# The end of the first attention's script: memory logits in pairs, values behind the last pair

## The chip, the core and the metric

The kernel runs on one core of one Trainium2 chip. Times are device microseconds (us) of one execution; the median of three runs is given. A core has TensorE (PE, with its weight loads PEld), VectorE (DVE), ScalarE (ACT), GpSimd (POOL) and SyncE (SP), which here issues the transfers. Each engine works through its own list of instructions in order and waits at semaphores for the others.

## The reference

A trunk of two layers over 512 tokens of width 1024. Layer 0 mixes tokens with differential attention (6 heads), layer 1 with gated linear attention. In both, 4 more heads attend to 256 memory tokens; both outputs are concatenated and go through one output projection. A gated MLP follows each layer. What the change touches is in layer 0:

```python
mix = diff_attention(q, k, v, ...)         # softmax(q0 k0) - lam * softmax(q1 k1), times v, per head
cross = memory_cross_attention(mem_q, ...) # below
x = x + jnp.concatenate([mix, cross], axis=-1) @ w_out[i]

def memory_cross_attention(q, mem, ...):   # q, k normalized per head
    logits = jnp.einsum('bqhd,bkhd->bhqk', q, k)
    p = jax.nn.softmax(logits, axis=-1)
    return jnp.einsum('bhqk,bkhd->bqhd', p, v)
```

## The kernel before

Large products are computed as three products of split operands (hi and lo parts, in fp32r), the attentions' small products in fp32. Activations are held transposed, in 128x512 tiles.

The order of PE's instructions is written out by hand; that of the other engines is made by a scheduler from the dependences. For the first attention the hand order is the string `SCRIPT`. `do` goes through its words. A letter with a number calls a step; a bare number lets `Filler` issue that many us of products from a queue: first the last projections (`gemm`, L329 to L331), then the first part of the output projection (`product`, L350 to L352, added to the residual on DVE by L1076). Costs of the filler are given by hand. Every step issues its PE instructions where it stands, so a step moved in the script is moved on PE.

The steps that matter, with the lines of the profile:

- `L`, with a step number 0 to 14: logits of one step of the differential attention (L736). A step holds one or two blocks of 128 queries of a head. DVE adds the bias and takes the maxima (L743), ACT exponentiates (L746), DVE combines the two softmaxes (L751 to L755). Steps 10 to 14 belong to the last pair of heads, 4 and 5.
- `T`: turns (transposes) such a step's weights on PE (L219); ACT copies them out of PSUM (L765). `V`: times the values (L777). When a head's last block is done, ACT squares its output (L788) for the norm.
- `s`, with a head's number: closes that norm and scales the output on DVE (L796). `F`: transposes the head's output (L219) and splits it on ACT (L309) and DVE (L310) into an operand of the output projection.
- `k0`, `k1`: transposes of the memory keys of layer 0 and of layer 1 (L219, copied by ACT, L577). `q1`: transposes of the memory queries (L219, copied by ACT, L599).
- `l`, with a block's number 0 to 3: memory logits of one block of 128 queries (L608), then its softmax: maxima on DVE (L616), four exponentials on ACT (L620), reciprocal and scaling on DVE (L622, L624). Each block gives two tiles of weights.
- `t`, with a tile's number 0 to 7: transposes of one of these tiles (L219), copied by DVE (even numbers) or ACT (odd ones), both L633.
- `v0`, `v1`: memory values for two blocks each (L646), 64 columns of the array at a time, and the split of the result (L309 and L310, tiles mxh and mxl). Each of these two operands of the output projection is whole only after `v1`.
- `O`: gives the filler the second part of the output projection, first those products that do not use head 5, of these first heads 3 and 4 (xsh, xsl) and then the memory heads (mxh, mxl). `!` empties the filler.

PSUM has eight banks, under four tags of two each: `mm` (projections), `lg`, `sm`, `tp` (transposes). A step that takes a bank waits on PE until the bank's former content has been read. Weights come through SP's transfers into raw tiles, are split by ACT (cast, L252) and DVE (L255) and held in six pairs of tiles; a pair is freed when the product that used it last has ended. The last projection before the output projection is that of layer 1's memory keys and values; ACT empties its banks (L568 and L569).

Of the kernel before, what the change touches and what calls it, by code (L numbers as in the profile page):

```python
# [48 lines left out]
    L9 V7 P4 b2 4.45 T8 T9 s2 3.0  # L49
    L10 V8 3.55 X P5 q0  # L50
    L11 b3 V9 T10 4.2
    L12 F2 V10 s3 T11 3.8 q1 k0
    L13 3.15 l0 V11 T12 3.65
    L14 F3 t0 3.3 V12 T13 t1 l1 3.9 T14 l2 t2 2.3 O k1 t3 s4 l3 v0 t4 V13 V14 t6 t5 1.3 t7 F4 v1 s5 F5 6.15 ! 4.55
"""

ORDER = (('v', 0), ('qk', 1), ('kv', 0), ('qk', 2), ('vm', 2), ('kv', 1))
# [28 lines left out]
def _pieces():  # L86

    plan = []

    def piece(key, name, i, ks, *ranges):  # L90
        plan.append((key, name, i, ks, ranges))

    for l in range(2):
        if l == 0:
            w = "w_in_diff"
            piece(("qk", 0), w, 0, K8, (0, 256), (768, 1024))
            for key in ORDER:
                if key[0] == "qk":
                    p = key[1]
                    piece(key, w, 0, K8, (256 * p, 256 * p + 256), (768 + 256 * p, 1024 + 256 * p))  # L100
                elif key[0] == "kv":
                    piece(key, "w_mem_kv", key[1], K8, (0, 512))
                elif key[0] == "vm":
                    p = key[1]
                    piece(key, w, 0, K8, (1536 + 256 * p, 1792 + 256 * p), (2304, 2560))
                else:
                    p = key[1]
                    piece(key, w, 0, K8, (1536 + 256 * p, 2048 + 256 * p))
        else:
            w = "w_in_gla"  # L110
            piece(("gm", 1), w, 0, K8, (2304, 2576))
            for c in range(5):
                piece(("g", c), w, 0, K8, (512 * c, min(512 * c + 512, 2304)))
        for i, part in enumerate(PASS[l]):
            for c, ks in part:
                piece(("o", l, i, c), "w_out", l, ks, (256 * c, 256 * c + 256))
        base = 0
        for nq in HALVES:
            for q in range(base, base + nq):
                piece(("ua", l, q), "w_up", l, K8, (256 * q, 256 * q + 256))  # L120
                piece(("ug", l, q), "w_up", l, K8, (DFF + 256 * q, DFF + 256 * q + 256))
            for c in range(4):
                piece(("dn", l, base, c), "w_down", l, tuple(range(2 * base, 2 * base + 2 * nq)),
                      (256 * c, 256 * c + 256))
            base += nq
    return plan


def _blocks():

    out = []
    for key, name, i, ks, ranges in _pieces():
        w = sum(b - a for a, b in ranges)
        step = WTILE // w
        out.append([(name, i, ks[j:j + step], ranges, w) for j in range(0, len(ks), step)])
    return out
# [42 lines left out]
def trunk(ctx, tc, head_d, x_t, mem_t, wpack, cols_a_d, cols_d, conv_d, gate_d, rel_bias, diff_lambda, consts, onehot, out):  # L179
# [12 lines left out]
    def bank(tag):  # L192
        return ps.tile([128, 512], F32, name=f"ps_{tag}", tag=tag)

    def xtile():
        return xs.tile([128, S], F32, name="xt", tag="xs", bufs=XS)
# [9 lines left out]
    def blk(b, w=128):  # L206
        return slice(w * b, w * b + w)
# [40 lines left out]
    plan, blocks, made = _pieces(), _blocks(), []  # L248
# [336 lines left out]
    class MemAttn:  # L585
# [13 lines left out]
                A.activation(self.qT[hp], p, AF.Copy, scale=c_mq(self.l))  # L599


        def logits(self, *blocks):
            banks = [(bank(tag), bank(tag)) for _, tag in zip(blocks, ("lg", "sm") if self.l else ("lg", "tp"))]
            for b, pl in zip(blocks, banks):
                for hp in range(2):
                    for j in range(2):
                        hh = blk(j, 64)
                        mm(pl[j][:, blk(hp, 256)], self.qT[hp][hh, blk(b)], kmT[self.l][hh, hp], start=True, stop=True)  # L608
            for b, pl in zip(blocks, banks):
                self.softmax(b, pl)  # L610
# [51 lines left out]
    def diff_layer(pool, mix, acc):  # L662
# [45 lines left out]
        def members(t):  # L708
            pr, s = divmod(t, len(TOGETHER))
            out, at = [], 0  # L710
            for j, i in TOGETHER[s]:
                out.append((2 * pr + j, i, 4 * j + i, at))
                at += 128 * (i + 1)
            return pr, out, at

        def bias(h):
            bt = heads[h]["bt"] = pool.tile([128, S], F32, name="bt", bufs=2)
            src = bass.AP(tensor=bias_d.tensor, offset=bias_d[h].offset + 1, ap=[[1, 128], [1, 512]])
            nc.sync.dma_start(bt, src)
            G.memset(bt[0:64, 0:64], -1e30)  # L720

        def logits(t, tag="lg"):
            pr, group, _ = members(t)
            P = pairs[pr]
            s2, nm, rc = P["s2"], P["nm"], P["rc"]
            for h, _, _, _ in group:
                if "bt" not in heads[h]:
                    bias(h)
            pls = bank(tag), bank(tag)
            for h, i, _, at in group:  # L730
                nk = 128 * (i + 1)
                cuts = (0, nk) if i == 0 else (0, nk // 2, nk)
                for k0, k1 in zip(cuts, cuts[1:]):
                    for m in range(2):
                        hh = blk(m, 64)
                        mm(pls[m][:, at + k0:at + k1], heads[h]["q"][hh, blk(i)], heads[h]["k"][hh, k0:k1],  # L736
                           start=True, stop=True)
            e = xtile(), xtile()
            for m in range(2):
                for h, i, g, at in group:  # L740
                    c = slice(at, at + 128 * (i + 1))
                    n1 = nm[:, 8 * m + g:8 * m + g + 1]
                    V.tensor_tensor_reduce(  # L743
                        out=e[m][:, c], in0=pls[m][:, c], in1=heads[h]["bt"][:, 127 + 128 * i::-1], scale=-1.0,
                        scalar=1e38, op0=ALU.add, op1=ALU.min, accum_out=n1)
                    A.activation(e[m][:, c], e[m][:, c], AF.Exp, scale=-1.0, bias=n1,  # L746
                                              accum_out=s2[:, m, g:g + 1])
            ids = sorted(g for _, _, g, _ in group)
            step = max(ids[-1] - ids[0], 1)
            b, lr = slice(ids[0], ids[-1] + 1, step), slice(8 + ids[0], 9 + ids[-1], step)  # L750
            V.reciprocal(rc[:, b], s2[:, 1, b])  # L751
            V.scalar_tensor_tensor(rc[:, lr], rc[:, b], nlam, s2[:, 0, b], op0=ALU.mult, op1=ALU.mult)
            for _, i, g, at in group:
                c = slice(at, at + 128 * (i + 1))
                V.scalar_tensor_tensor(e[1][:, c], e[1][:, c], rc[:, 8 + g:9 + g], e[0][:, c],  # L755
                                                    op0=ALU.mult, op1=ALU.add)
            live[t] = e[1]
# [57 lines left out]
        ma = MemAttn(pool, 0, qm, mix, False)  # L815
        ops, keys = [None] * 2, [None] * 2
        for key in ORDER:
# [16 lines left out]

        doing = {
            "L": logits, "M": lambda i: logits(i, "tp"), "T": turn, "V": values, "P": prepare, "F": finish,
            "N": lambda i: norms(i // 2, i % 2), "a": lambda i: ops[0]((2 * i, 2 * i + 1)),
            "b": lambda i: ops[1]((2 * i, 2 * i + 1)), "k": lambda i: keys[i]("sm"),
            "q": lambda i: ma.queries() if i else (F.need("v2"), ma.norm()),
            "l": lambda i: ma.logits(i), "t": ma.turn, "v": lambda i: ma.values(i, "sm"),  # L840
            "s": lambda i: scales.pop(i)(), "X": lambda i: load_x(x_t),
            "O": lambda i: last.append(out_proj(0, mix, 1, acc, 5)), "!": lambda i: F.flush()}
        do(SCRIPT, doing)
# [226 lines left out]
    def load_x(src):  # L1070
        for k in range(KT):
            xT[k] = xtile()
            nc.sync.dma_start(xT[k], src[k])
# [124 lines left out]
    for l in range(2):  # L1198
        with tc.tile_pool(name=f"at{l}", bufs=2) as pool:
            mix = [None] * 8  # L1200
            sums, acc = acc, [None]
            if l == 0:
                diff_layer(pool, mix, acc)
            else:
                gla_layer(pool, mix, sums)
                out_proj(1, mix, len(PASS[1]) - 1, acc)
                F.flush()
        with tc.tile_pool(name=f"ff{l}", bufs=2) as pool:
            acc = ffn(pool, l, acc)
# [73 lines left out]
```

## Time and profile before

| | |
|---|---|
| median of 3 runs | 1165.53 us (1165.47 to 1165.78) |
| profiled execution | 1165.97 us |
| its span, first to last instruction | 1164.1 us |
| DVE busy | 750.9 us (64%) |
| ACT busy | 545.5 us (47%) |
| stretch of the changed steps | about 172 to 226 us |

A row of a timeline gives the start, how long the instruction or the run of equal instructions took, the engine, the line, the operation, the tile written and those read, the shape, and how many there are; in brackets stands the engine's idle time before it and what ended it. Matmuls overlap with those behind them, so the step from one start to the next is what one costs on PE, and a row's own length is a little more. A matmul of fp32 stands as two records, one of fp32r or a transpose as one.

### The profile page before, as it was taken

The page shows a single profiled execution, that of the slowest core. Times are in us where ns is not written, and L with a number is a line of the kernel's source. Part 1 is how long each engine was busy: PE and PEld are TensorE (multiplying, and loading weights), DVE is VectorE, ACT ScalarE, POOL GpSimd, SP SyncE. Part 2 cuts the span into 40 slices and gives each one's busy share as a digit, 9 for nine tenths or more (in the row PEclk, how much of TensorE's full clock was granted, in tenths as well). Part 3 has the DMA queues.
Part 4 walks back from the last instruction along what each step waited for, and adds up shares of the span by engine and source line. Part 5 has one row for each costly group of instructions (what it writes and reads, how often), then busy time and mean ns, then how long its engine had stood idle before and what let it go on. Part 6 is the DMA issues. An engine that isn't in the chain of part 4 may idle for free.

```text
span 1164.1 us, 14796 instructions
## 1 busy us (share of the span) xinstructions
PE 1159.3 (100%) x5656; PEld 966.6 (83%) x5656; DVE 750.9 (64%) x1259; ACT 545.5 (47%) x951; POOL 6.5 (1%) x30
## 2 busy tenths in 40 slices
PE   9999999999999999999999999999999999999998
PEld 7888887888888888888888888988888888888887
DVE  7576778688677326677457637767976733576741
ACT  7676687555344213444337634436543421344420
POOL 0000000000000000000000000000000000000000
PEclk9999999999999999999999999999999999999999
DMA  8422242223223223222341220333332323231221
GB/s 298 162 81 85 77 140 73 72 102 130 76 91 125 83 84 125 73 95 98 121 145 60 99 100 7 114 118 104 105 112 73 108 92 109 90 110 73 91 100 45
DMA packets 39652, 117.76 MB, mean 101 GB/s; under 512 B 4767, under 2 KB 7256, under 8 KB 39582
## 3 DMA queue, kind: packets, MB, share of 16 engines
q1 hardware_dynamic: 39150, 116.44, 29.0%
q8 instruction: 44, 0.72, 0.2%
q10 hardware_dynamic: 432, 0.39, 0.1%
q14 instruction: 26, 0.21, 0.1%
HBM read 112.60 MB, written 4.21 MB: 100 GB/s over the span
## 4 chain that ended last, share of the span: by engine, by line
PE 99%; DMA 0%; ACT 0%; DVE 0%; DVEq 0%; issue 0%
PE ps_mm L350 9%; PE ps_mm L352 9%; PE ps_mm L351 9%; PE ps_sm L352 8%; PE ps_sm L350 8%; PE ps_sm L351 8%; PE ps_mm L329 6%; PE ps_mm L331 6%; PE ps_mm L330 6%; PE ps_tp L352 3%; PE ps_lg L352 3%; PE ps_lg L351 3%; PE ps_tp L351 3%; PE ps_lg L350 3%; PE ps_tp L350 3%; PE ps_tp L219 3%
## 5 line engine op out<-in xcount | busy, mean ns | idle before, releaser
L252 ACT CAST whi<-raw 128x1024 fp32r<-128x1024 f32 (+4 forms) x212 | 207.6, 986 | 247.1 <-PE ps_tp L351 120.9
L255 DVE TENSOR_TENSOR wlo<-raw,whi 128x1024 fp32r<-128x1024 f32 (+4 forms) x212 | 240.4, 1140 | 121.8 <-ACT whi L252 118.6
L350 PE MATMUL ps_mm<-xsh,whi 128*128 128x512 f32 x438 | 171.6, 392 | 0.0
L351 PE MATMUL ps_mm<-xsl,whi 128*128 128x512 f32 x438 | 170.5, 389 | 0.0
L352 PE MATMUL ps_mm<-xsh,wlo 128*128 128x512 f32 x438 | 170.5, 389 | 0.0
L350 PE MATMUL ps_sm<-xsh,whi 128*128 128x512 f32 x378 | 147.0, 389 | 0.0
L351 PE MATMUL ps_sm<-xsl,whi 128*128 128x512 f32 x378 | 147.0, 389 | 0.0
L352 PE MATMUL ps_sm<-xsh,wlo 128*128 128x512 f32 x378 | 147.0, 389 | 0.0
L329 PE MATMUL ps_mm<-whi,xsh 128*128 128x512 f32 (+2 forms) x328 | 126.5, 386 | 0.0
L1130 ACT ACTIVATE cvo<-u,cv 128x512 f32<-128x512 f32 x88 | 71.4, 815 | 112.1 <-DVE u L1128 112.1
L331 PE MATMUL ps_mm<-whi,xsl 128*128 128x512 f32 (+2 forms) x328 | 123.0, 375 | 0.0
L330 PE MATMUL ps_mm<-wlo,xsh 128*128 128x512 f32 (+2 forms) x328 | 122.8, 374 | 0.0
L351 PEld LDWEIGHTS ps_mm<-xsl,whi 128*128 128x128 f32 x438 | 82.3, 188 | 17.2 <-DVE xsl L310 0.4
L352 PEld LDWEIGHTS ps_mm<-xsh,wlo 128*128 128x128 f32 x438 | 82.2, 188 | 17.1
L350 PEld LDWEIGHTS ps_mm<-xsh,whi 128*128 128x128 f32 x438 | 82.2, 188 | 16.9 <-issue 0.3
L1131 DVE SCALAR_TENSOR_TENSOR cvo<-u,cv,cvo 128x512 f32<-128x512 f32 x88 | 65.7, 749 | 36.2 <-ACT cvo L1130 36.0
L351 PEld LDWEIGHTS ps_sm<-xsl,whi 128*128 128x128 f32 x378 | 70.9, 188 | 14.8
L352 PEld LDWEIGHTS ps_sm<-xsh,wlo 128*128 128x128 f32 x378 | 70.9, 188 | 14.7
L350 PEld LDWEIGHTS ps_sm<-xsh,whi 128*128 128x128 f32 x378 | 71.0, 188 | 14.7
L331 PEld LDWEIGHTS ps_mm<-whi,xsl 128*128 128x128 f32 x328 | 61.7, 188 | 11.4
L329 PEld LDWEIGHTS ps_mm<-whi,xsh 128*128 128x128 f32 x328 | 61.7, 188 | 11.0 <-issue 0.7
L330 PEld LDWEIGHTS ps_mm<-wlo,xsh 128*128 128x128 f32 x328 | 61.8, 188 | 10.0
(312 smaller groups left out, 1778.1 us busy)
## 6 DMA issues: line engine op xcount, KB each, us to landing
raw<-in_wpack_dram SPq DMA_DIRECT2D x178, 512.0 KB, 3.5
xt<-in_x_t_dram SPq DMA_DIRECT2D x15, 256.0 KB, 5.4
raw<-in_wpack_dram SPq DMA_DIRECT2D x15, 256.0 KB, 5.1
raw<-in_wpack_dram SPq DMA_DIRECT2D x8, 384.0 KB, 3.4
xres<-xt SPq DMA_DIRECT2D x8, 256.0 KB, 3.6
xt<-xres SPq DMA_DIRECT2D x8, 256.0 KB, 5.4
out_dram<-xt SPq DMA_DIRECT2D x7, 256.0 KB, 2.0
bt<-bias_d SPq DMA_DIRECT2D x6, 256.0 KB, 4.7
```

The lines of the kernel that those rows point to most:

```text
L219: nc.tensor.transpose(dst, src, ident[:n, :n])
L252: ins = A.copy(hi[:, c], raw[:, c])
L255: V.tensor_sub(lo[:, c], raw[:, c], hi[:, c].bitcast(F32))
L329: mm(p, sh[k][:, blk(b)], hi, start=k == 0, stop=False)
L330: mm(p, sh[k][:, blk(b)], lo, start=False, stop=False)
L331: mm(p, sl[k][:, blk(b)], hi, start=False, stop=k == KT - 1)
L350: mm(p, hi[:, blk(n)], bh, start=i == first, stop=False)
L351: mm(p, hi[:, blk(n)], bl, start=False, stop=False)
L352: mm(p, lo[:, blk(n)], bh, start=False, stop=i == last)
L1130: A.activation(c, u[:, 2:], AF.Identity, scale=cv[l][:, 2, j:j + 1], bias=cv[l][:, 3, j:j + 1])
L1131: V.scalar_tensor_tensor(c, u[:, 1:S + 1], cv[l][:, 1, j:j + 1], c, op0=ALU.mult, op1=ALU.add)
```

## The change

The last three lines of the script are written anew, and memory logits get a second form, `m`. A block takes two banks of one tag: of `lg` in the form `l`, of `tp` in the form `m`.

```diff
     L11 b3 V9 T10 4.2
-    L12 F2 V10 s3 T11 3.8 q1 k0
-    L13 3.15 l0 V11 T12 3.65
-    L14 F3 t0 3.3 V12 T13 t1 l1 3.9 T14 l2 t2 2.3 O k1 t3 s4 l3 v0 t4 V13 V14 t6 t5 1.3 t7 F4 v1 s5 F5 6.15 ! 4.55
+    L12 F2 V10 s3 T11 2.5 k0 q1 1.3
+    L13 m0 3.15 V11 T12 2.6 t0 t1 1.3
+    L14 m1 3.9 V12 F3 T13 1.3 s4 T14 1.3 k1 t2 F4 1.3 t3 0.65
+    l2 m3 O 1.3 v0 V13 V14 1.3 t4 t5 s5 1.95 t6 t7 F5 0.65 v1 ! 4.55
 """
...
-        def logits(self, *blocks):
-            banks = [(bank(tag), bank(tag)) for _, tag in zip(blocks, ("lg", "sm") if self.l else ("lg", "tp"))]
+        def logits(self, *blocks, tags=None):
+            banks = [(bank(tag), bank(tag)) for _, tag in zip(blocks, tags or (("lg", "sm") if self.l else ("lg", "tp")))]
...
-            "l": lambda i: ma.logits(i), "t": ma.turn, "v": lambda i: ma.values(i, "sm"),
+            "l": lambda i: ma.logits(i), "m": lambda i: ma.logits(i, tags=("tp",)),
+            "t": ma.turn, "v": lambda i: ma.values(i, "sm"),
```

So m0 and m1 stand right behind the logits of steps 13 and 14, m3 right behind l2. The transposes k0 and q1 stand ahead of the last six products of their projection, T12 to T14 and the turns t0 to t7 lie between products in another way, t6, t7 and F5 follow one another, and after v1 the emptied filler goes on at once.

## The prediction

> **What bounds the kernel now.** I read the page first, then the waits of TensorE (PE), then the windows around the changed stretch, 172 to 226 us, and last the timeline of each engine there. The page, its busy times and its chain of waits:
>
> ```profile
> span 1164.1 us, 14796 instructions
> PE 1159.3 (100%) x5656; PEld 966.6 (83%) x5656; DVE 750.9 (64%) x1259; ACT 545.5 (47%) x951; POOL 6.5 (1%) x30
> ...
> PE 99%; DMA 0%; ACT 0%; DVE 0%; DVEq 0%; issue 0%
> ```
>
> The waits of PE, whole (us in total, times, longest):
>
> ```profile
> PE ps_tp L456 <- DVE idle L451: 1.1, 1, 1.1
> ```
>
> The windows (length, busy time of PE, PEld, DVE, ACT and POOL, then granted clock, DMA share, GB/s):
>
> ```profile
> 172.00:195.00 23.00, 23.00 (x142) 18.57 (x141) 19.33 (x49) 17.26 (x49) 0.00 (x0) 1.00 0.20 67
> 195.00:226.00 31.00, 31.00 (x218) 25.88 (x217) 20.52 (x45) 15.63 (x51) 0.00 (x0) 1.00 0.13 43
> ```
>
> PE is busy for 1159.3 of 1164.1 us, the chain that ended last is 99% PE, and the only wait that the view of PE's waits shows in the whole run is 1.1 us at the start. In both windows PE is busy all the time at a granted clock of 1.00, while DVE and ACT have gaps. So the stretch costs what PE's instructions cost one after another. The change adds and removes no arithmetic, so it can gain only at the joints between PE instructions; and it loses whatever wait it opens.
>
> **What the reordering saves on PE.** The logits (L736, L608) use 64 rows of the array, two matmuls side by side. Into such a group and out of it PE loses time. Layer 1 has the paired form already, sixteen L608 records in a row:
>
> ```profile
> 185.98 0.39 PE L352 MATMUL ps_mm<-xsh,wlo 128*128 128x512 f32 x1
> 186.30 1.13 PE L736 MATMUL ps_lg<-kT,qT 64*128 64x256 f32 x8
> ...
> 193.59 1.13 PE L608 MATMUL ps_lg<-kmT,xt 64*128 64x256 f32 x8
> ...
> 194.99 0.39 PE L351 MATMUL ps_mm<-xsl,whi 128*128 128x512 f32 x1
> ...
> 636.25 1.13 PE L608 MATMUL ps_lg<-kmT,xt 64*128 64x256 f32 x8
> ...
> 638.52 0.40 PE L330 MATMUL ps_mm<-wlo,xsh 128*128 128x512 f32 x1
> ```
>
> Going in: products are 0.23 us apart, but 185.98 to 186.30 is 0.32, so 0.09. A lone group of eight records: 193.59 to the second product at 194.99 is 1.40, less that product's own 0.23, is 1.17. Sixteen: 638.52 - 636.25 - 0.23 = 2.04, so the second eight cost 0.87. Pairing saves 1.17 + 0.09 - 0.87 = 0.39 each. The change makes three pairs (m0 behind the L736 of step 13, m1 behind that of step 14, l2 with m3): 1.2. It gives back one joint, since the last logits stood directly ahead of v0 (L646) and no longer do: some 0.2 to 0.25, and up to 0.15 where a lone group stood between transposes, whose way out is cheaper than into products. I take 0.85, bounds 0.5 and 1.2.
>
> The Trainium skill (TensorEngine Tiling (Array Packing), Key Properties) says that a change of tiling mode drains the array while another tile in the same mode does not. The pair at 636.25, with other operands but the same 64 rows, bears it out; if every new operand drained as well, the sum below would be 0.85 us higher.
>
> **What it may uncover.** ACT and DVE run in order, and the changed program's order on them differs: each pair sends its exponentials (L620) down ACT together with those of the differential step. I follow each chain that ends in a PE instruction, with the durations of these rows.
>
> Wait 1, the second bank of the output projection (182.71 before). It takes the bank that the last memory-value product leaves, emptied on ACT by L568 and L569.
>
> ```profile
> 173.98 0.40 PE L331 MATMUL ps_mm<-whi,xsl 128*128 128x512 f32 x1
> ...
> 174.21 1.04 PE L219 MATMUL ps_tp<-C,qm 128*128 128x128 f32 x8
> ...
> 174.41 1.05 ACT L252 CAST whi<-raw 128x1024 fp32r<-128x1024 f32 x1 [0.53 <-PE ps_mm L331]
> ...
> 175.49 1.23 DVE L255 TENSOR_TENSOR wlo<-raw,whi 128x1024 fp32r<-128x1024 f32 x1 [0.61 <-ACT whi L252]
> ...
> 175.62 1.14 PE L736 MATMUL ps_lg<-kT,qT 64*128 64x192 f32 x12
> ...
> 177.39 0.62 ACT L746 ACTIVATE xt<-xt,nmd 128x384 f32<-128x384 f32 x1 [0.19 <-DVE nmd L743]
> ...
> 179.38 0.39 ACT L252 CAST whi<-raw 128x256 fp32r<-128x256 f32 x1
> ...
> 180.04 0.46 ACT L569 ACTIVATE vm<-ps_mm,r_mem 128x256 f32<-128x256 f32 x1
> ...
> 182.71 0.48 PE L350 MATMUL ps_mm<-xsh,whi 128*128 128x512 f32 x1
> ...
> 182.88 0.47 ACT L620 ACTIVATE xt<-ps_lg,nmm 128x256 f32<-128x256 f32 x1
> ...
> 184.69 0.60 ACT L765 COPY xt<-ps_tp 128x512 f32<-128x512 f32 x1
> ```
>
> Before, the cast L252 starts at 174.41, when the product at 173.98 has ended. The change puts the twelve transposes (0.11 each, 174.21 to 175.62 less the 0.09 of going in) ahead of the last six products: that product ends 1.32 later, the cast starts at 175.73, DVE's L255 behind it 1.08 later (as 174.41 to 175.49), at 176.81. The softmax of step 13 on DVE (L743) stands behind L255, 1.23 long; before, the first L746 on ACT came 0.67 after L255's end, so now at 178.71. From there to the 256-wide cast takes 1.99 as before (177.39 to 179.38): 180.70. But now four L620 stand ahead of that cast, 1.81 (182.88 to 184.69): 182.51. Cast, L568 and L569 take 1.12 (179.38 to 180.50): 183.63. PE itself arrives at 182.71 less 0.39 for one pairing, 182.32. That is a wait of 1.3, and a tenth less for each place where an instruction starts before its forerunner's end (rows overlap by nearly 0.1), so 1.1 to 1.4. I take 1.25. Before, the bank was empty at 180.50, 2.2 us early.
>
> A wait also has to be left. Here PE waited for DVE's xsl:
>
> ```profile
> 752.61 0.75 DVE L310 SCALAR_TENSOR_TENSOR xsl<-ps_tp,cols,xsh 128x512 fp32r<-128x512 f32 x1
> ...
> 753.42 0.50 PE L351 MATMUL ps_mm<-xsl,whi 128*128 128x512 f32 x1
> 753.75 0.40 PE L352 MATMUL ps_mm<-xsh,wlo 128*128 128x512 f32 x1
> ```
>
> DVE ends at 753.36, PE starts at 753.42, and the next product follows 0.33 later instead of 0.23: 0.06 + 0.10 = 0.16.
>
> Wait 2, the transposes of step 14 (T14). In the changed program their first one waits for ACT's copy (L765) of T13's, whose bank they take. T13 stands right behind V12 and F3, where ACT still has the four squares L788 of V12.
>
> ```profile
> 189.89 0.67 ACT L309 ACTIVATE xsh<-ps_tp,cols 128x512 fp32r<-128x512 f32 x1
> ...
> 191.73 1.05 PE L777 MATMUL ps_sm<-v,xt 128*128 128x128 f32 x8
> ...
> 192.37 0.37 ACT L788 ACTIVATE xt<-ps_sm,rs 128x128 f32<-128x128 f32 x1 [0.94 <-PE ps_sm L777]
> ...
> 193.76 0.60 ACT L765 COPY xt<-ps_tp 128x512 f32<-128x512 f32 x1
> ...
> 194.23 0.33 ACT L240 ACTIVATE rs_y<-ss,eps 128x4 f32<-128x4 f32 x1
> 194.43 0.60 ACT L633 COPY xt<-ps_tp 128x512 f32<-128x512 f32 x1
> ```
>
> From the start of V12's L777: ACT starts the squares 0.64 later, is through them at 2.03 (193.76), then xsh (L309, 0.67, of which 0.58 count because of the overlap), L240 (0.20 to the next start) and the copy, 0.60: 3.41, with the way out 3.57. PE: 0.89 for L777, 0.80 for eight transposes, 1.45 for six products: 3.14. Wait 0.43; I take 0.45, bounds 0.3 and 0.55.
>
> Wait 3, the transposes of F5. Now t6, t7 and F5 stand in a row, three banks' worth on two `tp` banks, so F5 waits for DVE's copy of t6.
>
> ```profile
> 198.88 0.60 PE L219 MATMUL ps_tp<-C,xt 128*128 128x128 f32 x4
> 199.51 0.59 ACT L765 COPY xt<-ps_tp 128x512 f32<-128x512 f32 x1 [0.29 <-PE ps_tp L219]
> ...
> 202.13 0.68 DVE L633 COPY xt<-ps_tp 128x512 f32<-128x512 f32 x1
> ```
>
> A copy starts 0.63 after the transposes' start (198.88 to 199.51) and takes 0.68 on DVE: 1.31, and 1.47 with the way out. PE comes after eight transposes, 0.87. Wait 0.6, bounds 0.5 and 0.7. Before, products stood between these transposes.
>
> Wait 4, the products of the memory heads' output (mxh, mxl), which now follow v1 directly; before, F5 and fifteen products (3.4 us) stood between.
>
> ```profile
> 209.82 0.38 ACT L309 ACTIVATE mxh<-ps_sm 128x256 fp32r<-128x256 f32 x1 [1.02 <-DVE mxl L310]
> ...
> 213.29 1.97 PE L646 MATMUL ps_sm<-xt,vm 128*64 128x128 f32 x32
> ...
> 215.19 0.66 PE L219 MATMUL ps_tp<-C,o 128*128 128x128 f32 x4
> ...
> 215.31 0.38 ACT L309 ACTIVATE mxh<-ps_sm 128x256 fp32r<-128x256 f32 x1 [1.17 <-PE ps_sm L646]
> ...
> 215.72 0.42 DVE L310 SCALAR_TENSOR_TENSOR mxl<-ps_sm,mxh 128x256 fp32r<-128x256 f32 x1 [0.59 <-ACT mxh L309]
> ```
>
> ACT starts mxh 0.12 after PE could go on (215.19); it ends at 215.69. PE starts at 215.75 and needs mxl, which ends at 216.14, so at 216.20, with 0.10 on the next. The second mxh waits for the first mxl (the releaser at 209.82): ACT 216.17 to 216.55, DVE 216.58 to 217.00, PE 217.06. Unhindered, that product (the fifth) would stand at 215.20 + 0.33 + 3 x 0.23 = 216.22; with the tenth for leaving it is 0.95 late. Bounds 0.8 and 1.1.
>
> The rest costs nothing: SP's list of transfers is the same row for row, casts that are up to 2 us later feed products more than 10 us on, and the earlier k0, F4 and s4 are single instructions in ACT's and DVE's gaps. PE's later arrivals do not shorten waits 2 to 4, since each of their chains starts at PE itself.
>
> **Sum.** 1.25 + 0.45 + 0.6 + 0.95 = 3.25, less 0.85: 2.4 us more. The profiled execution took 1165.97 (span 1164.1, 1.87 around it), 0.44 above the median of the runs; 1165.97 + 2.4 - 0.44 = 1167.9. With all bounds to one side 1.5 and 3.25, so about 1167.0 to 1168.8 for this case.
>
> **Rivals.**
> - A fifth wait. F5 needs head 5's `o`, which waits for V14's squares on ACT behind the mxh of v0, L240, L241 and a chain of small DVE steps. By my rows it is ready some 0.4 us before F5 would start, and behind wait 3; but 0.4 us over a dozen steps on two engines is thin. If these queues slip, as each hop of 0.03 to 0.06 allows, another 0.5 to 1.5 comes: 1168.4 to 1169.4.
> - Not slower: ACT is done in time at wait 1. What decides is whether L569 ends before PE arrives, 1.25 us earlier than I have it. Then 2.0 - 0.85 = 1.15 is left, 1166.7, within 0.2%. Against it: the four L620 stand ahead of the evacuation in ACT's order, and 1.81 us of work cannot vanish.
> - Nothing waits, so only the joints count: 1165.53 - 0.85 = 1164.7. It needs all four chains to be over a third shorter than their rows.
> - The clock falls after the waits. Both windows show 1.00. If it halved for the fifteen products behind one wait, 15 x 0.23 = 3.4 more: 1171.3. The Trainium skill (TensorE: Matmul & The Clock Gate, A second HAM failure mode: psum-queue depth-cycling) tells of a kernel whose short idle times between groups made the gate swing. No run here shows that yet, and four waits in 40 us are few.
>
> **How the numbers follow.** A measurement of this kernel can tell about 0.2%, 2.33 us, from no change, and the forecast lies right there. Forecast 0.60, of which 0.36 above 2.33 and 0.24 below; fifth wait 0.28; ACT in time 0.07; nothing waits 0.01; clock 0.03; and 0.01 for a gain past the bound, for which no row speaks. Slower 0.36 + 0.28 + 0.03 = 0.67, same 0.24 + 0.07 + 0.01 = 0.32, faster 0.01. The range leaves out the clock and the ends of the others: 1166.7 to 1169.4.
>
> **What would show it.** PE's waits should list four new ones: L350 for ACT (L569) near 182 us, over 1 us; L219 for ACT's L765 near 197; L219 for DVE's L633 near 216; L350 and L351 for mxh and mxl behind v1. The pairs L736 with L608 should show 0.87 for the second eight. It is wrong if PE shows no wait at L350, if F5 waits for `o`, or if products behind a wait lie more than 0.23 us apart.

## The result and the profile after

The changed kernel takes 1167.99 us (median of 11 runs, 1167.45 to 1170.54), beside 1165.78 for the kernel before in the 11 runs that go with them (1165.21 to 1167.43). The ratio is 1.002, with a 95% interval of 1.0012 to 1.0028: slower by 0.2%, or 2.2 us by the medians. Forecast were 1167.9 us and 2.4 us of loss. The profiled execution took 1167.99 too.

The page of the changed kernel (span, busy times, chain of waits) and, below it, the waits of PE, whole:

```profile
span 1166.2 us, 14789 instructions
PE 1159.4 (99%) x5656; PEld 965.9 (83%) x5656; DVE 751.3 (64%) x1259; ACT 546.7 (47%) x951; POOL 6.5 (1%) x30
...
PE 98%; ACT 1%; DVE 0%; DMA 0%; issue 0%; DVEq 0%
```

```profile
PE ps_tp L457 <- DVE idle L452: 1.1, 1, 1.1
PE ps_mm L351 <- ACT vm L570: 0.9, 1, 0.9
PE ps_mm L351 <- ACT mxh L310: 0.5, 1, 0.5
PE ps_tp L220 <- DVE xt L634: 0.3, 1, 0.3
PE ps_mm L532 <- ACT xsh L310: 0.2, 1, 0.2
```

PE is as busy as before (1159.4 beside 1159.3 us) in a span that is 2.1 us longer. Line numbers have moved by one: L351 was L350, L220 was L219. Of the new waits three stand in this view, the second one not; it shows on PE's weight load, below. The last row belongs to the first 5 us of the run.

**How large is the loss in one profile?** The time up to 153 us differs between executions, so spans are poor for tenths of a us. Two rows of PE, one ahead of the stretch and one behind it, are better: the first logits near 153 us, and the same product of the output projection near 233 us. Timelines of PE, before and after:

```profile
153.33 1.14 PE L736 MATMUL ps_lg<-kT,qT 64*128 64x192 f32 x12
...
232.70 0.39 PE L350 MATMUL ps_mm<-xsh,whi 128*128 128x512 f32 x1
```

```profile
153.03 1.14 PE L737 MATMUL ps_lg<-kT,qT 64*128 64x192 f32 x12
...
234.77 0.39 PE L351 MATMUL ps_mm<-xsh,whi 128*128 128x512 f32 x1
```

Before, 79.37 us lie between them, after 81.74: the stretch costs 2.37 more. Behind it the distance stays as it is to the end, so all of the loss is there. Every experiment below is measured so, most of them in a single run, and not all on one chip. That the measure can be trusted over runs and chips shows where no edit changes the amount of work: from the first row to the logits of step 13 all thirteen profiles take 22.29 or 22.30 us.

**The four waits.** Timeline of the changed kernel at wait 1 (start, duration, engine):

```profile
175.44 1.05 ACT L253 CAST whi<-raw 128x1024 fp32r<-128x1024 f32 x1
...
176.52 1.23 DVE L256 TENSOR_TENSOR wlo<-raw,whi 128x1024 fp32r<-128x1024 f32 x1 [1.93 <-ACT whi L253]
...
178.25 0.62 ACT L747 ACTIVATE xt<-xt,nmd 128x384 f32<-128x384 f32 x1 [1.77 <-DVE nmd L744]
...
180.25 0.46 ACT L621 ACTIVATE xt<-ps_tp,nmm 128x256 f32<-128x256 f32 x1
...
181.69 0.60 PE L220 MATMUL ps_tp<-C,xt 128*128 128x128 f32 x4
...
182.05 0.41 ACT L253 CAST whi<-raw 128x256 fp32r<-128x256 f32 x1
...
182.71 0.48 ACT L570 ACTIVATE vm<-ps_mm,r_mem 128x256 f32<-128x256 f32 x1
...
183.24 0.50 PE L351 MATMUL ps_mm<-xsh,whi 128*128 128x512 f32 x1 [0.95 <-ACT vm L570]
```

It is the chain of the forecast, link by link, each within 0.2 us of its forecast when counted from the row near 153: late product, late cast, DVE's L256, first exponential of step 13, four L621 of m0 ahead of the 256-wide cast, then the evacuation, which ends at 183.19. PE starts 0.05 behind it. Its transposes at 181.69 were through at 182.05 (four take 0.36 up to a product elsewhere), so the wait is 1.19.

Waits 2 and 3, in the same timeline:

```profile
197.39 0.60 ACT L766 COPY xt<-ps_tp 128x512 f32<-128x512 f32 x1
197.51 0.39 PE L353 MATMUL ps_mm<-xsh,wlo 128*128 128x512 f32 x1
...
198.04 0.42 PEld L220 LDWEIGHTS ps_tp<-C,xt 128*128 128x128 f32 x4 [0.56 <-ACT xt L766]
...
198.45 0.48 PE L351 MATMUL ps_mm<-xsh,whi 128*128 128x512 f32 x1
...
215.24 0.69 DVE L797 TENSOR_TENSOR o<-ps_sm,rs 128x512 f32<-128x512 f32 x1
...
215.48 1.03 PE L220 MATMUL ps_tp<-C,xt 128*128 128x128 f32 x8
216.12 0.69 DVE L634 COPY xt<-ps_tp 128x512 f32<-128x512 f32 x1 [0.18 <-PE ps_tp L220]
...
216.86 0.66 PE L220 MATMUL ps_tp<-C,o 128*128 128x128 f32 x4 [0.35 <-DVE xt L634]
...
217.27 0.48 PE L351 MATMUL ps_sm<-xsh,whi 128*128 128x512 f32 x1
```

T14 starts 0.53 after the product at 197.51 instead of 0.23, when ACT's copy (197.99) is done: 0.30, and its four transposes take 0.41 to the next product instead of 0.36: 0.35 in all. F5 starts at 216.86, when DVE's copy of t6 (216.81) is done; eight transposes from 215.48 take 0.87, so PE could have been there at 216.35: 0.51, and again 0.05 for leaving. Head 5's `o` (L797) was ready at 215.93, so the fifth wait did not come.

Wait 4:

```profile
218.15 1.97 PE L647 MATMUL ps_sm<-xt,vm 128*64 128x128 f32 x32
220.16 0.38 ACT L310 ACTIVATE mxh<-ps_sm 128x256 fp32r<-128x256 f32 x1 [1.92 <-PE ps_sm L647]
220.58 0.42 DVE L311 SCALAR_TENSOR_TENSOR mxl<-ps_sm,mxh 128x256 fp32r<-128x256 f32 x1 [1.55 <-ACT mxh L310]
220.60 0.49 PE L351 MATMUL ps_mm<-mxh,whi 128*128 128x512 f32 x1 [0.48 <-ACT mxh L310]
...
221.06 0.50 PE L352 MATMUL ps_mm<-mxl,whi 128*128 128x512 f32 x1
...
221.46 0.42 DVE L311 SCALAR_TENSOR_TENSOR mxl<-ps_sm,mxh 128x256 fp32r<-128x256 f32 x1 [0.45 <-ACT mxh L310]
...
221.94 0.50 PE L352 MATMUL ps_mm<-mxl,whi 128*128 128x512 f32 x1
...
222.28 0.39 PE L353 MATMUL ps_mm<-mxh,wlo 128*128 128x512 f32 x1
```

The first product waits for mxh (220.54), the second for mxl (221.00), the fifth, at 221.94, for the second mxl (221.88). A block of values takes 1.90 to its successor (213.29 to 215.19 in the kernel before), so PE could have gone on at 220.05, and the fifth product would have stood at 220.05 + 0.33 + 3 x 0.23 = 221.07. It was 0.87 late, and the product behind it follows 0.34 later instead of 0.23: 0.98.

The sum of the waits is 1.19 + 0.35 + 0.56 + 0.98 = 3.08. The stretch lost 2.37, so the joints saved 0.71.

### The profile page after: what moved, and what is told of

Same layout as the page of the kernel before. It is cut to its first block, busy times and chain, and to the rows that moved or that the text cites. A ratio compares the mean times of both kernels' runs of the same rounds, so it can differ in the third digit from the quotient of the medians.

```text
span 1166.2 us, 14789 instructions
## 1 busy us (share of the span) xinstructions
PE 1159.4 (99%) x5656; PEld 965.9 (83%) x5656; DVE 751.3 (64%) x1259; ACT 546.7 (47%) x951; POOL 6.5 (1%) x30
## 4 chain that ended last, share of the span: by engine, by line
PE 98%; ACT 1%; DVE 0%; DMA 0%; issue 0%; DVEq 0%
PE ps_mm L351 9%; PE ps_mm L352 9%; PE ps_mm L353 9%; PE ps_sm L352 8%; PE ps_sm L353 8%; PE ps_sm L351 7%; PE ps_mm L330 6%; PE ps_mm L332 6%; PE ps_mm L331 6%; PE ps_lg L352 3%; PE ps_tp L352 3%; PE ps_tp L353 3%; PE ps_tp L351 3%; PE ps_lg L353 3%; PE ps_lg L351 3%; PE ps_tp L220 3%
## 5 line engine op out<-in xcount | busy, mean ns | idle before, releaser
L256 DVE TENSOR_TENSOR wlo<-raw,whi 128x1024 fp32r<-128x1024 f32 (+4 forms) x212 | 240.4, 1140 | 121.1 <-ACT whi L253 120.3
L351 PE MATMUL ps_mm<-xsh,whi 128*128 128x512 f32 x438 | 172.0, 393 | 0.9 <-ACT vm L570 0.9
L351 PE MATMUL ps_sm<-xsh,whi 128*128 128x512 f32 x378 | 147.1, 389 | 0.0
L330 PE MATMUL ps_mm<-whi,xsh 128*128 128x512 f32 (+2 forms) x328 | 126.6, 386 | 0.0
L351 PEld LDWEIGHTS ps_mm<-xsh,whi 128*128 128x128 f32 x438 | 82.2, 188 | 18.5 <-ACT vm L570 1.2
L351 PEld LDWEIGHTS ps_sm<-xsh,whi 128*128 128x128 f32 x378 | 71.0, 188 | 14.8
L330 PEld LDWEIGHTS ps_mm<-whi,xsh 128*128 128x128 f32 x328 | 61.7, 188 | 11.2 <-issue 1.0
```

Of the source, the lines that this page charges most:

```text
L256: V.tensor_sub(lo[:, c], raw[:, c], hi[:, c].bitcast(F32))
L330: mm(p, sh[k][:, blk(b)], hi, start=k == 0, stop=False)
L351: mm(p, hi[:, blk(n)], bh, start=i == first, stop=False)
```

## The experiments

Three other theories stood beside the forecast's (four waits, each with its own chain, less what the joints save). A: there is one lateness of ACT and DVE, which begins at wait 1 and comes out again wherever PE next needs one of them. B and C: wait 1 is made by the pair alone, or by the late product alone. D: the pairs save less than their rows said. What was measured, with the starts of the two rows of PE:

| run | row near 153 | row near 233 | stretch against before |
|---|---|---|---|
| before | 153.33 | 232.70 | |
| changed | 153.03 | 234.77 | +2.37 |
| F5 behind three products | 152.83 | 233.98 | +1.78 |
| v1 earlier | 152.79 | 232.98 | +0.82 |
| products ahead of T14 | 152.85 | 234.19 | +1.97 |
| k0, q1 back, m0 single | 153.44 | 234.59 | +1.78 |
| k0, q1 back | 153.57 | 234.90 | +1.96 |
| m0 single | 153.05 | 234.30 | +1.88 |
| first two lines alone | 153.41 | 233.64 | +0.86 |
| all waits covered | 152.48 | 231.55 | -0.30 |
| the same without pairs | 152.61 | 232.45 | +0.47 |
| the same, t0 and t1 late | 152.81 | 231.90 | -0.28 |
| v0 behind the pair | 153.44 | 232.33 | -0.48 |

The edits are in the script; where nothing else is said, they are made to the changed kernel.

**Wait 3 alone.**

```diff
-    l2 m3 O 1.3 v0 V13 V14 1.3 t4 t5 s5 1.95 t6 t7 F5 0.65 v1 ! 4.55
+    l2 m3 O 1.3 v0 V13 V14 1.3 t4 t5 s5 1.95 t6 t7 0.65 F5 v1 ! 4.55
```

> Measure: what the stretch costs on PE against before (+2.36 us in the changed kernel: a PE row near 153 us and one near 233 us, difference of the two). Here the three products that stood between F5 and v1 stand ahead of F5. Theory (four waits of separate chains, less the saved joints): wait 3 (F5 for DVE's copy of t6) goes, the three products that cost 0.69 anyway now cover it, the others stay: +1.85 (2.36 less 0.51). Rival A (one late chain upstream that comes out wherever PE first needs it): F5 or v1 waits in its place, +2.3 to +2.4.

PE's waits in this run, whole:

```profile
PE ps_tp L457 <- DVE idle L452: 1.1, 1, 1.1
PE ps_mm L351 <- ACT vm L570: 0.9, 1, 0.9
PE ps_mm L351 <- ACT mxh L310: 0.5, 1, 0.5
```

The wait for DVE's copy is gone and nothing took its place; the others stand as they were. 0.59 came back, the wait with its slow leaving (0.56). Rival A falls here.

**Waits 3 and 4.**

```diff
-    l2 m3 O 1.3 v0 V13 V14 1.3 t4 t5 s5 1.95 t6 t7 F5 0.65 v1 ! 4.55
+    l2 m3 O 1.3 v0 V13 V14 1.3 t4 t5 s5 1.3 t6 t7 0.65 v1 0.65 F5 0.65 ! 4.55
```

> v1 stands three products behind t7, then three products, F5, three products, and only then the products of mxh and mxl. Theory: waits 3 and 4 both go, 2.36 - 0.51 - 0.97 = +0.9, up to 0.1 more where t4's successors now meet a bank too early. Rival A (the lateness of ACT and DVE comes from waits 1 and 2 and moves on): v1 waits for the copies of t6 and t7 instead, +1.5 or more.

1.55 came back (2.37 - 0.82); the two waits as read from the rows are 1.54.

**Wait 2.**

```diff
-    L14 m1 3.9 V12 F3 T13 1.3 s4 T14 1.3 k1 t2 F4 1.3 t3 0.65
+    L14 m1 3.9 V12 F3 T13 1.95 s4 T14 1.3 t2 F4 1.3 k1 t3
```

> Three products move from behind T14 to between T13 and s4, and k1 moves behind F4, so that T14 comes 0.69 later. Theory: wait 2 (T14 for ACT's copy of T13) goes, measured at 0.30 in the changed kernel; with k1's joint unchanged +2.05 (between 1.8 and 2.1). Rival A: +2.36, a wait of the same size at the next transposes.

0.40 came back, beside 0.35 from the rows. Waits 1, 3 and 4 stayed.

**Wait 1, both of its parts taken back.**

```diff
-    L12 F2 V10 s3 T11 2.5 k0 q1 1.3
-    L13 m0 3.15 V11 T12 2.6 t0 t1 1.3
+    L12 F2 V10 s3 T11 3.8 q1 k0
+    L13 0.65 m0 2.5 V11 T12 2.6 t0 t1 1.3
```

> k0 and q1 go back behind all six products of their projection, and m0 stands one group of three products behind the logits of step 13, no pair. Theory: the product whose evacuation PE waited for is early again and the four exponentials of m0 reach ACT later, so wait 1 (1.19) goes; the pair's joint is paid again (0.2 to 0.39). +1.35 to +1.6; waits 2, 3 and 4 stay as they are, within 0.05. Rival A (waits 2 to 4 are the lateness of wait 1 carried on): they shrink with it, +0.3 or less.

Only 0.59 came back, less than I had expected, though wait 1 is gone and waits 2 to 4 have their size. 1.19 less the pair's 0.39 should be 0.80. The missing 0.2 is a new wait that the view of waits doesn't list. Timelines of PE and DVE of this run, at step 14's pair:

```profile
188.07 1.13 PE L737 MATMUL ps_lg<-kT,qT 64*128 64x256 f32 x8
188.38 0.68 DVE L634 COPY xt<-ps_tp 128x512 f32<-128x512 f32 x1
...
189.03 1.22 PE L609 MATMUL ps_tp<-kmT,xt 64*128 64x256 f32 x8
...
190.18 0.50 PE L351 MATMUL ps_mm<-xsh,whi 128*128 128x512 f32 x1
```

In the changed kernel the same pair takes 1.93 (188.47 to 190.40), here 2.11. m1 takes two `tp` banks; the one of t0 is free only when DVE's copy (L634) ends at 189.06, 0.03 after the group has started on the other bank. In the single records of the trace the first two matmuls, which run side by side, start at 189.03 and 189.12, where in the changed kernel they start 0.01 apart; the later ones stay 0.02 apart. That is 0.18.

**One of the two parts back at a time.**

```diff
-    L12 F2 V10 s3 T11 2.5 k0 q1 1.3
+    L12 F2 V10 s3 T11 3.8 k0 q1
```

> Only k0 and q1 go back behind the six products; the pair of step 13 and m0 stays. Theory: wait 1 (1.19 at L351 for ACT's L570) goes, because the product and with it cast, L256 and the maxima of step 13 are 1.3 early again; but m0 now stands too close behind k0 and q1 and waits for ACT's copies of them, some 0.5 to 0.6 (one copy of 0.59 not covered). +1.6 to +1.8 in the stretch. Rival B (the pair itself causes wait 1, its four exponentials ahead of the evacuation, wherever k0 and q1 stand): L351 still waits 0.8 or more, +2.3 to +2.9.

```diff
-    L13 m0 3.15 V11 T12 2.6 t0 t1 1.3
+    L13 0.65 m0 2.5 V11 T12 2.6 t0 t1 1.3
```

> Only m0 moves, three products behind the logits of step 13; k0 and q1 stay early. Theory: both parts make wait 1, so taking the pair away leaves the late product: the exponentials of m0 come behind the 256-wide cast and the evacuation, the wait falls by 0.8 to 0.9 to some 0.35 and the pair's 0.39 is paid again: +1.8 to +1.95. Rival B (pair alone): the wait goes whole, 2.36 - 1.19 + 0.39 = +1.55. Rival C (the late product alone): the wait stays, +2.7.

Timeline of the run with k0 and q1 back, the pair at step 13 and ACT's end of the chain:

```profile
175.86 1.14 PE L737 MATMUL ps_lg<-kT,qT 64*128 64x192 f32 x12
176.19 1.26 ACT L600 ACTIVATE xt<-ps_tp,cols 128x512 f32<-128x512 f32 x2
...
178.56 0.53 PE L330 MATMUL ps_mm<-whi,xsh 128*128 128x512 f32 x1
...
182.08 0.47 ACT L570 ACTIVATE vm<-ps_mm,r_mem 128x256 f32<-128x256 f32 x1
```

and of the run with m0 single, with PE's weight load for T12:

```profile
180.92 0.46 ACT L570 ACTIVATE vm<-ps_mm,r_mem 128x256 f32<-128x256 f32 x1
...
181.24 1.05 PE L778 MATMUL ps_sm<-v,xt 128*128 128x128 f32 x8
...
182.33 0.42 PEld L220 LDWEIGHTS ps_tp<-C,xt 128*128 128x128 f32 x4 [0.23 <-ACT xt L621]
182.34 0.66 PE L220 MATMUL ps_tp<-C,xt 128*128 128x128 f32 x4
```

Counted from the row near 153 us, the evacuation L570 ends at 30.16 in the changed kernel (183.19 - 153.03), and PE would have come at 29.02 (183.24 - 1.19 - 153.03). With k0 and q1 back it ends at 28.98, 1.18 earlier; with m0 single at 28.33, 1.83 earlier, which is the four exponentials (1.81 in the forecast). So each part taken back alone removes the wait at L351, and B and C fall both: the wait is the sum of the two, past what the bank had to spare. With k0 and q1 back, 28.98 is only just in time for a PE that comes at 29.02; in this run PE comes later still, because of what this version costs instead. m0 is held up close behind q1's copies on ACT (L600), as expected, but the pair takes 2.70 instead of 1.94 (175.33 to 177.27 in the changed kernel), 0.76 lost where I had 0.5 to 0.6; the total is +1.96, outside the expected +1.6 to +1.8. With m0 single no wait is left at the bank, where I had placed one of 0.35. Instead T12's transposes at 182.34 start 0.22 later than eight L778 at 0.11 would have it: they take a `tp` bank of m0, whose exponentials (L621, the releaser in the row) now come later on ACT. So the total of +1.88 lies in the range expected by luck, with another wait than the one I had placed.

**The first two lines of the change alone**, as an edit of the kernel before:

```diff
-    L12 F2 V10 s3 T11 3.8 q1 k0
-    L13 3.15 l0 V11 T12 3.65
+    L12 F2 V10 s3 T11 2.5 k0 q1 1.3
+    L13 m0 3.15 V11 T12 3.65
     L14 F3 t0 3.3 V12 T13 t1 l1 3.9 T14 l2 t2 2.3 O k1 t3 s4 l3 v0 t4 V13 V14 t6 t5 1.3 t7 F4 v1 s5 F5 6.15 ! 4.55
```

> The kernel before with the first two parts of the change alone: k0 and q1 early, m0 paired with step 13; everything from step 14's logits on in the old order. Theory: wait 1 at full size, 1.19, less one saved pair 0.39: +0.8 to +0.9, and nothing behind it. Rival A (one lateness that comes out again at each later point): waits behind it too, +1.2 to +2.4.

+0.86 as expected, and behind wait 1 PE waits nowhere in the stretch. So waits 2 to 4 do not follow from wait 1.

**All waits covered, with pairs and without.** These four lines in place of the changed kernel's:

```diff
+    L12 F2 V10 s3 T11 3.8 q1 k0
+    L13 0.65 m0 2.5 V11 T12 1.3 t0 t1 2.6
+    L14 m1 3.9 V12 F3 T13 1.95 s4 T14 1.3 t2 F4 1.3 k1 t3
+    l2 m3 O 1.3 v0 V13 V14 1.3 t4 t5 s5 1.3 t6 t7 0.65 v1 0.65 F5 0.65 ! 4.55
```

> All four waits covered by work that stands there anyway, two pairs kept (step 14 with m1, l2 with m3): k0 and q1 back and m0 single, t0 and t1 three products earlier, T14, k1, v1 and F5 as in the runs that did one of these. Theory (the parts add, since each wait has its own chain): 2.36 - 0.80 (m0 single; 1.19 less the pair's 0.39) - 0.40 (T14 with k1) - 1.55 (waits 3 and 4) = -0.4 in the stretch, between -0.5 and -0.2, so a little under the kernel before; as a time 1165.4 beside 1165.8, too small for the rounds to tell from no change. Rival A (a lateness that always comes out somewhere): a wait is left, above 0 in the stretch.

and with `L14 0.65 m1 3.25` and `l2 0.65 m3 O 0.65 v0` in it instead of the two pairs:

> As the run with all waits covered, but with three products between step 14's logits and m1, and three between l2 and m3: the arithmetic and the order else are the same. It measures what two pairs save where no wait hides it. Theory: 2 x 0.39 = 0.78 more than with the pairs. Rival D (the joints save less than the rows said, as the sum of the changed kernel seems to ask: 2.97 of waits less 2.36 is 0.6 for three pairs and a lost joint): 0.4 more or less.

and with `T12 1.95 t0 t1 1.95`:

> As the run with all waits covered, but t0 and t1 stand one group of three products later, closer to the pair of step 14 and m1, which takes the bank of t0. Theory: if DVE's copy of t0 is late only where it stood in the run with m0 single, this is the same within 0.05; if DVE's copy of t0 lies behind L256 and the layer norm's products whatever its place on PE, the second half of the pair is out of step again by about 0.2.

PE's waits of the first of these runs, whole:

```profile
PE ps_tp L457 <- DVE idle L452: 1.1, 1, 1.1
```

The sum of the parts was -0.4 and -0.30 is measured; the parts add. With and without the two pairs differ by 0.77 (0.47 + 0.30), 0.385 a pair. So D falls: a pair saves what its rows say. With t0 and t1 later the stretch is the same within 0.02, so the half-filled pair was a matter of that one place. As a time this kernel has 1165.53 us beside 1165.76 for the kernel before, ratio 0.9998 (0.9989 to 1.0007): no difference that these runs can tell.

**The joint that was given back.** The kernel before had v0 directly behind its last logits. In the last experiment it stands so again:

```diff
-    l2 m3 O 1.3 v0 V13 V14 1.3 t4 t5 s5 1.3 t6 t7 0.65 v1 0.65 F5 0.65 ! 4.55
+    l2 m3 v0 O 1.3 V13 V14 1.3 t4 t5 s5 1.3 t6 t7 0.65 v1 0.65 F5 0.65 ! 4.55
```

> The run with all waits covered, with one thing moved: v0 stands directly behind the pair of l2 and m3, O's six products behind v0, as the kernel before had v0 behind its last logits. Theory (a joint between two kinds of matmul costs by what stands on both sides): pair to product 0.097 + 0.11 and product to v0 0.095 fall away against pair to v0 0.10, so 0.2 less: -0.5 in the stretch (-0.306 there). Rival E (the joint of logits to v0 costs as much as both joints with products): -0.3. Rival A: v0 waits for DVE's or ACT's copies, above -0.3. As a time 0.5 below the kernel before, 1165.3, at the edge of what the rounds can tell.

Timelines of PE, first with all waits covered, then with v0 behind the pair:

```profile
204.08 0.50 PE L351 MATMUL ps_mm<-xsh,whi 128*128 128x512 f32 x1
204.41 0.40 PE L352 MATMUL ps_mm<-xsl,whi 128*128 128x512 f32 x1
...
205.34 0.39 PE L353 MATMUL ps_mm<-xsh,wlo 128*128 128x512 f32 x1
205.66 1.97 PE L647 MATMUL ps_sm<-xt,vm 128*64 128x128 f32 x32
```

```profile
204.06 1.05 PE L609 MATMUL ps_tp<-kmT,xt 64*128 64x256 f32 x8
205.04 1.97 PE L647 MATMUL ps_sm<-xt,vm 128*64 128x128 f32 x32
206.94 0.50 PE L351 MATMUL ps_mm<-xsh,whi 128*128 128x512 f32 x1
```

With products between, the first one behind the pair takes 0.33 to the next instead of 0.23, and the last one ahead of v0 0.32. Both tenths are gone with v0 directly behind the pair: -0.48 beside -0.30, 0.18 for 0.2 expected. Rival E falls. This is the best version found: 1165.26 us beside 1166.00, ratio 0.9992 (0.9983 to 1.0001). Its stretch is 0.48 us shorter than before; as a time it can't be told from the kernel before.

## Why the prediction was right

| term | forecast | measured |
|---|---|---|
| wait 1, evacuation behind m0's exponentials | 1.25 | 1.19 |
| wait 2, T14's bank | 0.45 | 0.35 |
| wait 3, F5's bank | 0.6 | 0.56 |
| wait 4, mxh and mxl | 0.95 | 0.98 |
| joints | -0.85 | -0.71 |
| sum | 2.4 | 2.37 |

- The path was read rightly: with PE busy all the time, only joints could gain, and each new wait came out one to one. All four are where the forecast put them, end 0.05 to 0.06 before PE starts, and name the releaser it named; undone (2 alone, 3 alone, 3 with 4), they gave back their own size within 0.05.
- Wait 1 was followed over five hops of ACT and DVE with rows of before, and was 0.06 off. That both a late product and the exponentials ahead of the evacuation were needed for it was not said in the forecast, but its sum had both terms (1.32 and 1.81), and the runs show that each alone stays within what the bank had to spare, the exponentials only just.
- Wait 2 was mis-sized by 0.1. The term was worked out as 0.43 and taken as 0.45. ACT's chain and PE's arrival came out as forecast within 0.03 (PE stood 0.30 instead of 0.33); but leaving the wait, 0.10 behind a product in the forecast, costs 0.05 where transposes follow.
- The joints were mis-sized by 0.14. The 0.39 a pair was right (0.385 measured where nothing waits; in the changed kernel l2 with m3 takes the 2.04 of layer 1's pair, 206.12 - 203.85 - 0.23). Too small was what is given back: 0.35 in the forecast, 0.46 here (3 x 0.39 - 0.71). Of it 0.18 is v0's lost place behind the logits, which was measured by itself. That the value blocks now lead into products instead of transposes, and that lone logits stood beside transposes before, is my reading of the rest. Rows agree with it: before, four transposes behind a lone group take 0.49 (187.37 to 187.86) instead of 0.44, where a product takes 0.34 instead of 0.23; now the product behind V14 takes 0.32 (211.07 to 211.39). No run took it apart.
- The waits came out 0.17 smaller and the saving 0.14 smaller. These errors cancel to 0.03, so the sum is better than its terms, by luck. So is the time, 0.1 us off: it starts from 1165.53 for the kernel before, which has 1165.78 in the runs beside the changed one, and the loss by medians is 2.2 instead of 2.4.
- The fifth wait did not come. `o` was ready at 215.93, 0.42 before PE could have started F5 without wait 3 (216.35). The forecast had a margin of 0.4 and distrusted it; behind wait 3 the margin is 0.93 (216.86).
- The granted clock was 1.0 over the whole run, and behind a wait products lie 0.23 apart as ever, from the second one on. The Trainium skill (TensorE: Matmul & The Clock Gate, A second HAM failure mode: psum-queue depth-cycling) describes another kernel, in which short idle times of PE between groups make the gate swing; waits of 0.3 to 1.2 us, four in 40 us, did not do it here.

The ratio of 1.002 lies on the border of 0.2% that the forecast had named as what a measurement can tell.

## What to carry to other kernels

Where one engine is busy all the time, write down for each step that is moved ahead of others who empties the bank that the bound engine takes next, and count everything that now stands ahead of that one instruction in its engine's order; a bank with 2.2 us to spare was lost to two moves, each of which alone leaves it in time. A saved mode change is worth what its rows say, but look at what stands on both sides of the joint, since 0.2 of 0.39 us goes back when the neighbour changes. Steps that take the same pair of banks (here three blocks of transposes in a row) need work between them that takes none.

## What the hardware showed besides

- The start of the run differs from execution to execution. Up to the logits near 153 us all these kernels are the same on PE, yet that row stands between 152.48 and 153.57 in thirteen profiles. Most of it is there by the first L330 (L329 in the kernel before), at 27.93 to 28.79; more comes near 102 us, where in some profiles PE waits for ACT's copies of kT (0.4 us at the most in the view of waits, in the run with v0 behind the pair). Such a spread of 1.1 us is half of what the change costs, and is why two rows of one trace tell more here than spans do.
- Matmuls that run side by side can lose their step: where the bank of one half came free 0.03 behind the start of the other, that half started 0.09 behind it, the group of eight took 0.18 longer, and the view of waits lists nothing for it.
